# First weights on ScalarE's queue, attention's bias and the identity behind the first loads, twelve products of ones at the start of a hybrid decoder layer

## The chip, the core and the metric

The kernel runs on one core of one Trainium2 chip (trn2). The core has TensorE (matrix products into PSUM), VectorE (DVE), ScalarE (ACT), GpSimd (POOL) and SyncE (SP), which here only issues transfers; 16 DMA engines move data between the device's memory and SBUF. Each engine runs its own list of instructions in order and waits on semaphores for the others. The metric is the time of one execution in microseconds (us), the median of the runs.

## What is computed

One layer of a decoder on x with 2048 positions and 1024 channels, float32 throughout. Cut to what matters here:

```python
h = rmsnorm(x, norm1_g)
z = h @ w_in            # columns: q | k | v | conv a, gate | lru gate, x
y_attn = attention_mixer(q, k, v)      # 6 heads, three dilated windows, ALiBi bias
y_conv = conv_module(...)              # GLU, causal depthwise conv of 31 taps, LayerNorm, swish
y_lru  = recurrent_mixer(...)          # gated linear recurrence
x = x + concat(y_attn, y_conv, y_lru) @ w_out
x = x + square(relu(rmsnorm(x, norm2_g) @ w_up)) @ w_down
return rmsnorm(x, final_g)
```

## The kernel before, in words

The 2048 positions are done in two halves of 1024. For each half the input projection runs (`inproj`), then the three mixers, the output projection and the two large products of the MLP. Tensors lie with channels on the 128 partitions. A float32 product is made of three products of rounded parts: every operand is split by `split` into a rounded high part (ScalarE, a cast or a scaled copy, lines 235 and 238) and a low part (VectorE, lines 236 and 239), and `products` (lines 255, 258, 261) multiplies high by high, high by low and low by high. Each such product is 128 rows by 512 columns.

`inproj(0)` begins the program. x arrives as eight rows of 128 channels (k = 0 to 7), each in two blocks of 512 positions (256 KB, line 329), the weights as blocks of 128 x 512 (256 KB, line 244 in `load_w`). All of these pass through five raw buffers in turn (`raw_tile`), so that a load waits until the block that had its buffer is split. The split weights go to a ring of eight tiles (`wide_ring`), so that a cast can wait for TensorE to be done with older weights. The first group of `project` multiplies three column tiles of w_in with all eight rows: 18 products for each row k, into six PSUM banks. Beside the split, ScalarE squares each block (lines 266 and 269) and VectorE adds the squares (line 270); when row 6 comes up, `norm` multiplies these sums with the matrix `ones_d` (line 279, a plain float32 product), and square root (line 351), reciprocal (line 352) and the evacuation of the banks (line 381) follow. Only then can the second group have its bank.

The first weight block is asked for by `acts.between`, which the first pass of `Acts.more` calls once, after the first activation block. The order of the rest on each engine is set by a scheduler that knows the program's order and the priorities given in it; `tc.issue_after` holds an instruction behind another.

Ahead of `inproj`, `body` loads `vec` (all small vectors), sets `ones_d` on GpSimd and a few constants. `project_v` (line 397 on) loads the identity for transposes (`ident`, line 399); it is used first there, at line 404. `setup` prepares the recurrence's small weights and a polynomial on VectorE (lines 217 to 231). `attention` takes its bias (the ALiBi slopes and masks, 128 x 512) from `consts` by `bias_of` (line 644) on GpSimd's queue, and then the first unit's queries, keys and values by `fetch_keys` (lines 591, 606, 610), which come back from the device's memory (`zscr`, `vscr`) and so wait for their stores. The bias is added to the scores at line 711 on VectorE. The taps of the convolution (line 462) run on VectorE in the same stretch.

Of the kernel before, what the change touches and what calls it, by code (L numbers as in the profile page):

```python
# [77 lines left out]
def body(tc, xt, w_in, w_v, w_out, w_up, w_down, vecs, lru_wa, lru_wx, consts, out):  # L78
# [114 lines left out]
    def v(name, i=0, n=1):  # L193
        at = VEC[name][0] + i
        return vec[:, at:at + n]

    def setup():
        for m, w in enumerate((lru_wa, lru_wx)):
            raw = wide_tile()[:, :3 * P]
            nc.gpsimd.memset(raw, 0.0)  # L200
            for t in range(3):
                for j in range(2):
                    nc.sync.dma_start(raw[j * HD:(j + 1) * HD, t * P + j * HD:t * P + (j + 1) * HD], w[2 * t + j])
            gh, gl = X(22)[:, m * 3 * P:(m + 1) * 3 * P], X(23)[:, m * 3 * P:(m + 1) * 3 * P]
            split(raw, gh, gl)
            for part, a in ((m, gh), (2 + m, gl)):
                nc.sync.dma_start(gates_w.rearrange("t p n -> p t n")[:, :, part * P:(part + 1) * P],
                                  a.bitcast(F32).rearrange("p (t n) -> p t n", t=3))
        zero = cst.tile([P, 32], F32, name="zero")
        nc.gpsimd.memset(zero, 0.0)  # L210
        for t in range(2):
            nc.sync.dma_start(uscr[t][:, 0:32], zero)
        for t in range(3):
            nc.sync.dma_start(lscr[t][:, 0:32], zero)
        lam = v("lru_lambda", 0, 3)
        w = [splus[:, 3 * i:3 * i + 3] for i in range(5)]
        nc.scalar.activation(w[0], lam, AF.Abs)
        nc.scalar.activation(w[0], w[0], AF.Exp, scale=-1.0)
        nc.vector.tensor_scalar(w[1], w[0], 2.0, None, op0=OP.add)
        nc.vector.reciprocal(w[1], w[1])  # L220
        nc.vector.tensor_tensor(w[0], w[0], w[1], OP.mult)
        nc.vector.tensor_tensor(w[1], w[0], w[0], OP.mult)
        nc.vector.memset(w[2], 1.0 / 19)
        for n in range(17, 0, -2):
            nc.vector.tensor_tensor(w[2], w[2], w[1], OP.mult)
            nc.vector.tensor_scalar(w[2], w[2], 1.0 / n, None, op0=OP.add)
        nc.vector.scalar_tensor_tensor(w[2], w[2], 2.0, w[0], op0=OP.mult, op1=OP.mult)
        nc.vector.tensor_scalar(w[3], lam, -1.0, 0.0, op0=OP.mult, op1=OP.max)
        nc.vector.tensor_add(w[2], w[2], w[3])
        nc.vector.tensor_scalar(w[3], w[2], 8.0, None, op0=OP.mult)  # L230
        nc.vector.tensor_scalar(w[4], w[2], -8.0, None, op0=OP.mult)
# [6 lines left out]
            nc.scalar.activation(h, raw, AF.Copy, scale=scale)  # L238
            nc.vector.scalar_tensor_tensor(l, raw, scale, h.bitcast(F32), op0=OP.mult, op1=OP.subtract)

    def load_w(src):
        n = src.shape[-1]
        raw = raw_tile()[:, :n]
        nc.sync.dma_start(raw, src)
        h, l = wide_ring()[:, :n], wide_ring()[:, :n]
        split(raw, h, l)
        return h, l
# [48 lines left out]
    def project(src, group, acts, nk, evac, hook=None):  # L296
        banks = [[main_bank() if i < 2 else mix_bank() for _ in range(2)] for i in range(len(group))]
        w = {}
        if not len(acts):
            acts.between = lambda: w.update({0: load_w(src(group[0], 0))})  # L300
        for k in range(nk):
            while len(acts) < k + 1:
                acts.more()
            if hook is not None and k == hook[0]:
                hook[1]()
            for i, t in enumerate(group):
                if k % 4 == 0 and (k or i not in w):
                    w[i] = load_w(src(t, k // 4))
                products(banks[i], w[i], k % 4, acts[k], k == 0, k == nk - 1)
            while len(acts) < (min(k + 2, nk) if k < 4 else nk):  # L310
                acts.more()
        for i, t in enumerate(group):
            evac(t, banks[i])
# [3 lines left out]
    def inproj(h, after=None):  # L317
# [78 lines left out]

        def project_v():
            if h == 0:
                nc.sync.dma_start(ident, consts[:, 6 * 256:])
            nc.sync.dma_start(rscr[tok].rearrange("(a n) -> a n", a=1), r1[0:1, :])  # L400
            rows = raw_tile()[0:8, 0:P]
            nc.sync.dma_start(rows, rscr[tok].rearrange("(c p) -> c p", p=P))
            bank = (main_bank if h else conv_bank)()
            nc.tensor.transpose(bank[:, 0:HS // P], rows, ident[0:8, 0:8])
            nc.scalar.copy(rcol[h], bank[:, :HS // P])
            for c0 in range(0, HS // P, 4):
                banks = [main_bank()[:, :VW] for _ in range(4)]
                for k in range(KT):
                    wh, wl = load_w(w_v[k])
                    ah, al = acts[k]  # L410
                    for i, bank in enumerate(banks):
                        c = slice((c0 + i) * P, (c0 + i + 1) * P)
                        nc.tensor.matmul(bank, ah[:, c], wh, start=k == 0, stop=False)
                        nc.tensor.matmul(bank, ah[:, c], wl, start=False, stop=False)
                        nc.tensor.matmul(bank, al[:, c], wh, start=False, stop=k == KT - 1)
                for i, bank in enumerate(banks):
                    c = c0 + i
                    if i % 2 == 0:
                        z = z_tile()
                    o = z[:, i % 2 * NB:i % 2 * NB + VW]  # L420
                    nc.vector.tensor_scalar(o, bank, rcol[h][:, c:c + 1], None, op0=OP.mult)
                    nc.sync.dma_start(vscr[h * HS + c * P:h * HS + (c + 1) * P, :], o)
# [158 lines left out]
    def fetch_keys(h, g, bt, half):  # L581
        load = attn_loads(h).dma_start
        c0 = h * HS + bt * NB + half * 256
        back = (P, NB, HS)[g]
        own = slice(c0, c0 + 256)
        lead = 0 if c0 < back else P if g == 0 else 256
        width = lead + 256
        raw = mtile()[:, :NB]
        for a in range(2):
            ap = slice(a * HD, (a + 1) * HD)  # L590
            load(raw[ap, :].rearrange("p (j n) -> p j n", j=2), zscr[Q_T + g][:, own].rearrange("(j p) n -> p j n", j=2))
        lows = []
        for j in range(2 if lead else 1):
            kl = mtile_r()[:, :width if lead else NB]
            lows.append(kl)
            rows = slice(j * HD, (j + 1) * HD)
            for a in range(2):
                dst = kl[a * HD:(a + 1) * HD, :].bitcast(F32)
                if g == 0 and lead:
                    load(dst, zscr[K_T + g][rows, c0 - lead:c0 + 256])  # L600
                elif lead:
                    at = c0 // back * back
                    src = zscr[K_T + g][rows, at - back:at + back].rearrange("p (b n) -> p b n", b=2)
                    load(dst.rearrange("p (b n) -> p b n", b=2), src[:, :, c0 - at:c0 - at + 256])
                else:
                    load(dst.rearrange("p (j n) -> p j n", j=2), zscr[K_T + g][:, own].rearrange("(j p) n -> p j n", j=2))
        vv = mtile()[:, :width]
        vc = slice(g * P, (g + 1) * P)
        if g == 0:
            load(vv.rearrange("p (b c) -> p b c", c=P), vscr[c0 - lead:c0 + 256, vc].rearrange("(b p) c -> p b c", p=P))  # L610
        else:
            for at, t in ((lead, 0),) + (((0, back),) if lead else ()):
                dst = vv[:, at:at + 256].rearrange("p (u c) -> p u c", u=2)
                if g == 1:
                    base = h * HS + bt * NB - t
                    src = vscr[base:base + NB, vc].rearrange("(s r) c -> s r c", r=4)
                    load(dst, src[:, 2 * half:2 * half + 2, :])
                else:
                    base = h * HS - t
                    src = vscr[base:base + HS, vc].rearrange("(s r e) c -> s r e c", r=8, e=2)  # L620
                    at_r = bt * 4 + half * 2
                    for e in range(2):
                        load(dst[e * HD:(e + 1) * HD], src[:, at_r:at_r + 2, e, :])
        return raw, lows, vv, lead
# [13 lines left out]
    def attention(h):  # L638
# [3 lines left out]
        def bias_of(g):  # L642
            b = mtile()[:, :NB]
            attn_loads(h).dma_start(b, consts[:, g * NB:(g + 1) * NB])
            return b

        bias = bias_of(0)
        got = fetch_keys(h, *sets[0])
        yield 0
        yield 0  # L650
        qs, keys, vv, lead = split_keys(*got)
# [977 lines left out]
```

## Time and profile before

| | us |
|---|---|
| median of 3 runs | 2007.19 |
| the three runs | 2004.91, 2007.19, 2007.31 |
| profiled execution | 2004.13 |
| its span, first to last instruction | 2002.3 |
| TensorE busy in the span | 1953.0 (98%) |
| VectorE busy | 1447.3 (72%) |
| ScalarE busy | 1041.1 (52%) |

All rows come from the one profiled execution; its times count from the span's start. In the rows PE is TensorE and PEld its weight load, DVE is VectorE, ACT ScalarE, POOL GpSimd and SPq the queue of SyncE. L255 is line 255 of the kernel before. `raw<-in_xt` names the written and the read tensor. The end of a product is modelled, since products overlap in the array; the distance from one start to the next is what TensorE needs for one. Behind an arrow stands what ended the engine's idle time.

### The profile page before, as it was taken

What the parts mean: (1) busy time and instruction counts of PE and PEld (TensorE: products, weight loads), DVE (VectorE), ACT (ScalarE), POOL (GpSimd) and SP (SyncE); (2) the same over time, 40 slices, a digit from 0 to 9 for tenths busy, and PEclk for the clock granted to TensorE, in tenths of its full rate; (3) what the DMA queues carried; (4) which work ended last, traced back from release to release, by engine and by line L of the source; (5) the groups of instructions that cost most, each with busy time, mean ns of one, the idle gap of its engine ahead of it and who ended that gap; (6) DMA issues with size and microseconds to landing.
All of it is one profiled execution on the core that took longest, in us unless ns stands there. A gap on an engine that the chain in (4) does not pass through costs nothing.

```text
span 2002.3 us, 25415 instructions
## 1 busy us (share of the span) xinstructions
PE 1953.0 (98%) x8876; PEld 1588.9 (79%) x8876; DVE 1447.3 (72%) x1961; ACT 1041.1 (52%) x1606; POOL 168.0 (8%) x296
## 2 busy tenths in 40 slices
PE   8999999999999999999999999999999999999996
PEld 6887777877777777888888888787888887888885
DVE  7899783589667666878879899767556555577885
ACT  6144872453557764555565666345555546444441
POOL 0023100100022413000000000100000000000001
PEclk9999999999999999999999999999999999999999
DMA  5555595743656647545888687754444437776773
GB/s 169 164 151 162 168 300 180 245 138 111 202 158 182 194 146 235 176 153 178 277 290 297 208 301 241 241 189 142 148 147 158 150 139 266 250 281 211 273 233 125
DMA packets 201851, 399.51 MB, mean 200 GB/s; under 512 B 25366, under 2 KB 33798, under 8 KB 201660
## 3 DMA queue, kind: packets, MB, share of 16 engines
q1 hardware_dynamic: 182308, 341.49, 50.9%
q0 software_dynamic: 16208, 45.91, 7.7%
q10 hardware_dynamic: 3208, 10.49, 1.5%
q8 instruction: 70, 1.15, 0.2%
q14 instruction: 57, 0.47, 0.1%
HBM read 287.21 MB, written 119.00 MB: 203 GB/s over the span
## 4 chain that ended last, share of the span: by engine, by line
PE 73%; DMA 9%; DVE 9%; ACT 5%; issue 3%; POOL 0%; SPq 0%; DVEq 0%; ACTq 0%; POOLq 0%
PE bank L1120 9%; PE bank L1121 9%; PE bank L1122 9%; PE bank L1419 8%; PE bank L1421 8%; PE bank L1420 8%; PE mm L255 3%; PE mm L261 3%; PE mm L258 3%; PE bank L933 2%; PE bank L935 2%; PE bank L934 2%; DVE rounded L893 1%; DVE wide L462 1%; DMA second<-in_w_down 1%
## 5 line engine op out<-in xcount | busy, mean ns | idle before, releaser
L1120 PE MATMUL bank<-rounded,pair 128*128 128x512 f32 x896 | 353.0, 394 | 3.4 <-ACT low L1129 1.7
L1121 PE MATMUL bank<-rounded,pair 128*128 128x512 f32 x896 | 349.3, 390 | 0.0
L1122 PE MATMUL bank<-rounded,pair 128*128 128x512 f32 x896 | 349.1, 390 | 0.0
L1419 PE MATMUL bank<-rounded,rounded 128*128 128x512 f32 x736 | 288.0, 391 | 2.0 <-DVE z L1432 0.9
L1421 PE MATMUL bank<-rounded,rounded 128*128 128x512 f32 x736 | 286.7, 390 | 1.5 <-DVE rounded L893 1.5
L1420 PE MATMUL bank<-rounded,rounded 128*128 128x512 f32 x736 | 286.4, 389 | 0.0
L893 DVE TENSOR_TENSOR rounded<-rounded 128x1024 fp32r<-128x1024 f32 (+1 forms) x172 | 186.8, 1098 | 74.7 <-ACT rounded L892 73.9
L892 ACT CAST rounded<-rounded 128x1024 fp32r<-128x1024 f32 (+1 forms) x172 | 160.5, 948 | 133.1 <-DMA rounded<-fscr 94.9
L1120 PEld LDWEIGHTS bank<-rounded,pair 128*128 128x128 f32 x896 | 168.2, 188 | 41.4 <-issue 3.0
L1122 PEld LDWEIGHTS bank<-rounded,pair 128*128 128x128 f32 x896 | 168.2, 188 | 35.2 <-issue 0.2
L1121 PEld LDWEIGHTS bank<-rounded,pair 128*128 128x128 f32 x896 | 168.3, 188 | 34.0 <-issue 0.7
L255 PE MATMUL mm<-rounded,rounded 128*128 128x512 f32 x496 | 160.0, 397 | 11.2 <-ACT rounded L235 7.6
L1419 PEld LDWEIGHTS bank<-rounded,rounded 128*128 128x128 f32 x736 | 138.2, 188 | 33.4 <-issue 1.9
L1421 PEld LDWEIGHTS bank<-rounded,rounded 128*128 128x128 f32 x736 | 138.1, 188 | 31.3 <-DVE rounded L893 2.3
L1420 PEld LDWEIGHTS bank<-rounded,rounded 128*128 128x128 f32 x736 | 138.1, 188 | 29.1 <-issue 0.5
L261 PE MATMUL mm<-rounded,rounded 128*128 128x512 f32 x496 | 159.1, 396 | 0.0
L892 ACT CAST rounded<-kept 128x1024 fp32r<-128x1024 f32 x80 | 84.0, 1050 | 144.1 <-DVE kept L1288 72.3
L258 PE MATMUL mm<-rounded,rounded 128*128 128x512 f32 x496 | 157.1, 394 | 0.0
L235 ACT CAST rounded<-raw 128x512 fp32r<-128x512 f32 (+1 forms) x96 | 55.6, 583 | 150.2 <-PE mm L258 92.5
L892 ACT CAST pair<-wraw 128x1024 fp32r<-128x1024 f32 x64 | 67.4, 1053 | 120.0 <-PE bank L1121 113.5
L893 DVE TENSOR_TENSOR rounded<-kept,rounded 128x1024 fp32r<-128x1024 f32 x80 | 97.9, 1223 | 38.4 <-ACT rounded L892 38.0
L893 DVE TENSOR_TENSOR pair<-wraw,pair 128x1024 fp32r<-128x1024 f32 x64 | 78.2, 1222 | 63.2 <-ACT pair L892 61.0
(327 smaller groups left out, 3618.6 us busy)
## 6 DMA issues: line engine op xcount, KB each, us to landing
fscr<-low SPq DMA_DIRECT2D x224, 256.0 KB, 2.1
rounded<-fscr SPq DMA_DIRECT2D x112, 512.0 KB, 4.1
second<-in_w_down SPq DMA_DIRECT2D x80, 512.0 KB, 5.5
kept<-in_w_down SPq DMA_DIRECT2D x48, 512.0 KB, 5.0
raw<-in_w_in SPq DMA_DIRECT2D x64, 256.0 KB, 3.8
low<-in_w_up SPq DMA_DIRECT2D x64, 256.0 KB, 3.2
wraw<-in_w_up SPq DMA_DIRECT2D x64, 256.0 KB, 2.9
raw<-in_xt SPq DMA_DIRECT2D x32, 256.0 KB, 3.7
```

The lines of the kernel that those rows point to most:

```text
L235: nc.scalar.copy(h, raw)
L255: nc.tensor.matmul(bank, wh[:, sl], ah[:, cols], start=first_, stop=False)
L258: nc.tensor.matmul(bank, wh[:, sl], al[:, cols], start=False, stop=False)
L261: nc.tensor.matmul(bank, wl[:, sl], ah[:, cols], start=False, stop=last_)
L892: nc.scalar.copy(h, raw)
L893: nc.vector.tensor_sub(l, raw, f32(h))
L1120: nc.tensor.matmul(bank, wh[:, sl], hi(x), start=fresh and k == 0, stop=False, **kw)
L1121: nc.tensor.matmul(bank, wh[:, sl], lo(x), start=False, stop=False, **kw)
L1122: nc.tensor.matmul(bank, wl[:, sl], hi(x), start=False, stop=k == KH - 1, **kw)
L1419: nc.tensor.matmul(banks[j], th[:, c], sh[:, x], start=fresh and k0, stop=False, **kw)
L1420: nc.tensor.matmul(banks[j], th[:, c], sl[:, x], start=False, stop=False, **kw)
L1421: nc.tensor.matmul(banks[j], tl[:, c], sh[:, x], start=False, stop=k1, **kw)
```

## The change

`body` gets twelve products of `ones_d` with itself (128 columns each, plain float32) into the bank of `conv_bank`, ahead of everything else on TensorE. `load_w` is cut in two: `load_raw` takes a buffer and issues the load on a given queue, and the first weight block is asked for on ScalarE's queue before the activations are, so that it also takes the first raw buffer. The load of the identity is held behind the last activation load. In `attention`, the first bias is asked for after the first unit's `fetch_keys`, and held behind GpSimd's last instruction so far; this holds for both halves.

```diff
+    warm = conv_bank()
+    for _ in range(12):
+        nc.tensor.matmul(warm[:, :P], ones_d, ones_d, start=True, stop=True)
...
+    def load_raw(src, queue):
+        raw = raw_tile()[:, :src.shape[-1]]
+        queue.dma_start(raw, src)
+        return raw
+
+    def load_w(src, raw=None):
         n = src.shape[-1]
-        raw = raw_tile()[:, :n]
-        nc.sync.dma_start(raw, src)
+        if raw is None:
+            raw = load_raw(src, nc.sync)
...
         if not len(acts):
-            acts.between = lambda: w.update({0: load_w(src(group[0], 0))})
+            raw = load_raw(src(group[0], 0), nc.scalar)
+            acts.between = lambda: w.update({0: load_w(src(group[0], 0), raw)})
...
             if h == 0:
-                nc.sync.dma_start(ident, consts[:, 6 * 256:])
+                with tc.issue_after(last_x[0].ins):
+                    nc.sync.dma_start(ident, consts[:, 6 * 256:])
...
-        bias = bias_of(0)
         got = fetch_keys(h, *sets[0])
+        with tc.issue_after(next(i for i in reversed(nc.cur_bb.bb.instructions) if i.engine == mybir.EngineType.Pool)):
+            bias = bias_of(0)
```

On ScalarE at the start of the program, before (`raw_99` and `raw_101` are the two blocks of row 0, `raw_100` the first weights; line 235 casts weights, line 238 rounds activations):

```order
L183 ACT_TABLE_LOAD
L183 ACTIVATE ones_cr<-ones_d 128x128
L217 ACTIVATE splus<-vec 128x3
L218 ACTIVATE splus<-splus 128x3
L238 ACTIVATE rounded_77<-raw_99,vec 128x512
L266 ACTIVATE row_104<-raw_99 128x512
L235 CAST rounded_83<-raw_100 128x512
L238 ACTIVATE rounded_77<-raw_101,vec 128x512
```

The same place now (`raw_99` holds the first weights, `raw_100` and `raw_101` row 0; lines 239 and 242 are the former 235 and 238):

```order
L247 DMA raw_99<-in_w_in 128x512
L183 ACT_TABLE_LOAD
L183 ACTIVATE ones_cr<-ones_d 128x128
L221 ACTIVATE splus<-vec 128x3
L239 CAST rounded_83<-raw_99 128x512
L242 ACTIVATE rounded_77<-raw_100,vec 128x512
L275 ACTIVATE row_104<-raw_100 128x512
L242 ACTIVATE rounded_77<-raw_101,vec 128x512
```

The weights' load stands first, their cast ahead of the first activation block, and the second small operation of `setup` has moved behind the blocks.

On GpSimd around the first attention unit's fetch, before (`in_consts` is the bias):

```order
L210 MEMSET zero 128x32
L644 DMA m<-in_consts 128x512
L591 DMA m<-zscr 64x2x256 x2
L606 DMA mr<-zscr 64x2x256 x2
L610 DMA m<-vscr 128x2x128
L591 DMA m<-zscr 64x2x256 x2
```

The same place now (lines 602, 617, 621 and 655 are the former 591, 606, 610 and 644):

```order
L214 MEMSET zero 128x32
L602 DMA m<-zscr 64x2x256 x2
L617 DMA mr<-zscr 64x2x256 x2
L621 DMA m<-vscr 128x2x128
L655 DMA m<-in_consts 128x512
L602 DMA m<-zscr 64x2x256 x2
```

The bias has moved from the head of the queue to behind the fetch of the values.

## Rows read from the trace of the kernel before

**Rows 1.** The page, busy time of TensorE; then shares of the chain.

```profile
PE 1953.0 (98%) x8876; PEld 1588.9 (79%) x8876; DVE 1447.3 (72%) x1961; ACT 1041.1 (52%) x1606; POOL 168.0 (8%) x296
...
PE 73%; DMA 9%; DVE 9%; ACT 5%; issue 3%; POOL 0%; SPq 0%; DVEq 0%; ACTq 0%; POOLq 0%
```

**Rows 2.** The chain in order of time, 0 to 60: start, us, what.

```profile
2.12 5.57 DMA raw<-in_xt
...
8.49 0.80 PE mm L255
9.29 0.85 PE mm L258 x2
...
14.29 0.47 PE mb L258 x2
...
15.22 0.47 PE mm L255 x2
...
35.65 0.86 PE mb L279 x2
...
45.86 0.47 PE mm L255
```

**Rows 3.** Timeline, 0 to 16: start, us, engine, line, operation, idle before.

```profile
0.74 0.20 POOL L182 MEMSET ones_d<- 128x128 f32 x1 [0.29 <-POOLq L1621]
...
1.72 0.68 POOL L644 DMA_DIRECT2D m<-in_consts  x1
...
5.48 0.72 ACT L238 ACTIVATE rounded<-raw,vec 128x512 fp32r<-128x512 f32 x1 [2.23 <-DMA raw<-in_xt]
6.11 0.61 ACT L266 ACTIVATE row<-raw 128x512 f32<-128x512 f32 x1
...
6.63 0.60 ACT L235 CAST rounded<-raw 128x512 fp32r<-128x512 f32 x1
...
7.07 8.12 SPq L329 DMA_DIRECT2D raw<-in_xt  x8
...
7.28 0.28 PEld L255 LDWEIGHTS mm<-rounded,rounded 128*128 128x128 f32 x1 [7.28 <-ACT rounded L235]
7.28 0.79 PE L255 MATMUL mm<-rounded,rounded 128*128 128x512 f32 x1 [7.28 <-ACT rounded L235]
...
10.60 0.72 ACT L238 ACTIVATE rounded<-raw,vec 128x512 fp32r<-128x512 f32 x1 [0.61 <-DMA raw<-in_xt]
...
12.77 0.75 DVE L239 SCALAR_TENSOR_TENSOR rounded<-raw,vec,rounded 128x512 fp32r<-128x512 f32 x1
```

**Rows 4.** Windows: length, busy (instructions) of PE, PEld, DVE, ACT, POOL; granted clock, DMA.

```profile
10.00:11.00 1.00, 1.00 (x4) 0.81 (x3) 0.98 (x3) 0.40 (x1) 0.00 (x0) 1.00 0.72 219
16.00:17.00 1.00, 1.00 (x6) 0.84 (x5) 1.00 (x3) 1.00 (x3) 0.00 (x0) 1.00 0.72 213
100.00:150.00 50.00, 49.97 (x273) 40.43 (x273) 46.09 (x82) 21.72 (x53) 11.98 (x21) 1.00 0.52 152
150.00:200.00 50.00, 49.28 (x248) 37.42 (x247) 46.80 (x82) 21.68 (x59) 17.47 (x29) 1.00 0.55 161
200.00:250.00 50.00, 48.26 (x237) 37.17 (x236) 36.37 (x72) 43.01 (x80) 9.33 (x16) 1.00 0.57 169
```

**Rows 5.** DMA, 0 to 10: rate in 40 slices; issues with us to landing.

```profile
GB/s 0 0 0 0 0 0 0 149 64 107 180 180 115 115 172 139 229 270 188 164 270 311 385 402 377 377 410 385 393 414 361 299 256 262 195 189 221 320 229 148
...
m<-in_consts POOLq DMA_DIRECT2D x1, 256.0 KB, 5.5
...
vec<-in_vecs SPq DMA_DIRECT2D x1, 58.0 KB
```

**Rows 6.** Timeline, 32 to 36: the last sums of squares.

```profile
34.01 1.29 DVE L270 TENSOR_TENSOR row<-row,tmp 128x512 f32<-128x512 f32 x2
```

**Rows 7.** Timelines of GpSimd and VectorE: third fetch of the first unit, first bias.

```profile
97.84 0.72 POOL L610 DMA_DIRECT2D m<-vscr  x1 [12.94 <-DMA vscr<-z]
...
101.00 0.28 DVE L711 CUSTOM_DVE_ANT_0 m<-mb,m 128x128 f32<-128x128 f32 x1
```

More of the change, by code (lines that the diff above doesn't have):

```diff
@@ L239, in split @@
             nc.vector.scalar_tensor_tensor(l, raw, scale, h.bitcast(F32), op0=OP.mult, op1=OP.subtract)
-    def load_w(src):
+    def load_raw(src, queue):
[3 more added lines that the diff above has]
+    def load_w(src, raw=None):
         n = src.shape[-1]
-        raw = raw_tile()[:, :n]
-        nc.sync.dma_start(raw, src)
+        if raw is None:
+            raw = load_raw(src, nc.sync)
         h, l = wide_ring()[:, :n], wide_ring()[:, :n]
```

## The prediction

> **What bounds the kernel now.** I read the page first: TensorE is busy for 98% of the span of 2002.3 us, and of the chain that ended last 73% is TensorE [rows 1]. So time is lost or won only where TensorE stands still or runs slowly, and the change works at the one place where it does both, the start. The chain in order of time shows it [rows 2]: it begins with the landing of the second half of the first activation block (issued at 2.12, 5.57 us on the way), then TensorE takes over at 8.49 and keeps the chain almost without a break to the second group of products at 45.86. From 9.29 two products of 512 columns take 0.85 us, 0.427 each, which is 512 columns at 1.2 GHz; from 14.29 they take 0.47 and soon 0.45, the 2.4 GHz level. The granted clock of the windows says 1.00 in both stretches, but 4 products start in the us from 10 and 6 in the us from 16 [rows 4]: here the level is read from the spacing, not from that column. TensorE had stood for 7.28 us, made one product, waited again, and then run back to back since 8.49 when the level rose.
>
> The timeline gives the order of arrival [rows 3]: the first activation block is rounded on ScalarE at 5.48, the first weights behind it at 6.63, the first product at 7.28. The second activation row is issued at 7.07, lands at 10.60, and its last low part is done by VectorE at 12.77 + 0.75 = 13.5. At the slow level TensorE reaches that row only at 15.22 [rows 2], 1.7 us after it was ready: TensorE, not the data, set the pace.
>
> **Part 1, first weights on ScalarE's queue; bias and identity away from the start.** Before, vec (58 KB), the first block, its weights, the bias (256 KB, landed 1.72 + 5.5 = 7.2) and three further blocks share the DMA engines, and about 585 KB have moved by 5.25 (the first 21 slices of the rate row, a quarter us each) [rows 3, 5]. After, the first 570 KB are vec, first weights and first activation block alone. At the same rates both have landed by 5.25; the weights are issued at about 0.74, where ScalarE now starts with a table load, so I take 4.9 for them and 5.3 for the block. ScalarE casts the weights (0.60) to 5.5 and rounds the block (0.72) to 6.2 [rows 3]: first product at 6.25, against 7.28. The bounds are 5.6 (all landed at 4.3) and 6.9 (both at 5.5, as the first block now).
>
> The Trainium skill speaks against more: in "Trainium Kernel Development and Optimization", Key Constraints, it says that transfers issued from several engines' queues run on the same 16 DMA engines and interleave, so a second queue saves issue time only. By that rule weights and block would land together at about 5.3 and the first product would be at 6.65; the sum below would lose 0.4 us.
>
> The buffer of the first weights takes the second activation row next. It is free at 4.9 + 0.60 + 0.75 = 6.25, against 7.07 now; with the 3.53 us from issue to use of now [rows 3] the row is there at 9.8. Round, square, round (0.72, 0.61 to 0.65, 0.72) end at 11.9, VectorE's low part at 12.65. Small set-up operations are pushed behind the blocks on VectorE; they have no reader near, and I cost them at nothing.
>
> **Part 2, the twelve products of ones.** A plain f32 product of 512 columns takes 0.86 at the fast level [rows 2], so one of 128 columns 0.215, or 0.43 at the slow one. Twelve last 2.6 to 5.2 us. They wait for ones_d alone (0.74 + 0.20 [rows 3]) and so end between 3.5 and 6.1, ahead of the first product at 6.25, and PSUM's bank is next used far behind. Now the level rose after 5.4 us of unbroken work. If it rises for the ones as it did for the products, products run at 0.228 from the start. 18 products per row then take 4.1 us: TensorE would be through the first row at 10.4, and at 10.7 with the third weights' cast. It waits for the second row: two products from 11.95 and the low part at 12.65 make that row start effectively at 12.2. Now it is 15.22: **3.0 us earlier**.
>
> **What is late next.** Row 7 of the first group waits for the sums of squares: VectorE ends them at 34.01 + 1.29 = 35.3 [rows 6], and TensorE arrives at 35.65 [rows 2], with almost no slack. TensorE at 15.22 - 3.0 would arrive at 32.65. Are the sums ready? Their last activation block uses a buffer that a weight block frees, and that weight's cast waits for TensorE to let go of a weight tile; this limb moves by the 3.0. The activations' own stream on ScalarE and VectorE moves by 13.5 - 12.65 = 0.85 only, so the sums come between 32.3 and 34.45, and the product of the sums moves by 1.2 to 3.0. I take 2.4, nearer to the upper end because the last block is freed by weights. From that product to the next group (square root, reciprocals, evacuation; 35.65 to 45.86 [rows 2]) nothing is changed, so the 2.4 us reach the second group.
>
> **Part 3, bias and identity behind.** The identity goes out behind the last activation load, some 50 us ahead of its first use: nothing. GpSimd asked for the bias at 1.72 and stood idle after; now it asks behind the third fetch of the first unit, which was issued at 97.84 after waiting 12.94 for vscr [rows 7]. So it goes out at 97.84 + 0.72 - 2.4 = 96.2 and lands 3.5 (like an activation row) to 5.5 us later, 99.7 to 101.7. VectorE's first use was at 101.00; in the new order it stands behind one more conv tap (about 1.3 us), so it is wanted at 99.9. VectorE stands 0 to 1.8 us. It is busy 46.1 of 50 us there [rows 4] and TensorE waits for nothing: I cost it at nothing, with up to 1.8 in the range. On TensorE the first attention products move back by a few dozen products and the two orders agree again some 590 products in (about 130 us). The second half's bias is asked for over 100 us ahead of its use.
>
> **The sum.** -2.4 us (-1.2 to -3.0; with the bias, +0.6 to -3.0), all on the chain. The profiled execution took 2004.13, which would become 2001.7. It is 3.1 us under the median of the runs, 2007.19, and the three timed runs average 2006.5; from that: **2004.1 us**. What this kernel's measurement can tell from no change is about 0.2%, 4 us.
>
> **Rivals.**
> - *The ones don't raise the clock.* They keep TensorE busy only in short records; the row for it would be 0.427 spacing after the first product. Then the first row takes 18 x 0.427 = 7.7 from 6.25, the second row starts at about 14.3, 0.9 earlier: 2005.6. For it: one product at 7.28 and a wait did not raise it [rows 2, 3]. Against: twelve in a row are unbroken. In "TensorE: Matmul & The Clock Gate", Part 1, the Trainium skill says that the number of slow products differs from run to run and isn't to be fitted; no single trace here can show that.
> - *The bias comes late* (ends slower). VectorE stands in order before the casts' low parts and evacuations, so TensorE is held. For it: the bias was there some 94 us ahead and now has hardly any slack. Against: VectorE's stall comes to 1.8 us at the bounds above. It decides from the point where the bias lands 2.4 us behind the 99.9 at which it is wanted (6.1 us after its issue) and all of that reaches TensorE: then the gain is gone. At 3.1 us behind, the time is 2006.5 + 0.7 = 2007.2.
> - *The ones overrun* (also slower). If each record paid its weight load and its stream one after the other at the slow level (0.28 [rows 3] + 0.21, 24 records), they would end at 12.8, the second row would start at 16.9, 1.7 later: 2008.2. Against: loads of 0.28 hide behind products now.
> - *More is won later.* TensorE idles 0.7 and 1.7 us in 150 to 250 [rows 4], waiting on attention; the new order may close most of it: 2002.1.
>
> **How the numbers follow.** Forecast 0.57, clock stays slow 0.15, bias late 0.08, overrun 0.08, more won later 0.12. The forecast's own range is 2002.3 to 2005.9 (its bounds and about 1 us of scatter). To leave out no more than 2 in 10, the range reaches from 2001.4 to 2007.4. Faster by over 0.2% is below 2003.2: a third of the forecast (0.19) and nearly all of the last rival (0.11), 0.30. Slower by over 0.2% is above 2011.2: only an overrun worse than priced, 0.03. Within: 0.67.
>
> **What would show it.** Right: spacing of 0.228 at the first products, first product at 5.6 to 6.9, second row at about 12.2, sums' product at 32.6 to 34.5, second group at 43 to 44.7, and all later stages as much earlier. Wrong: 0.427 after 8 us; ones that end behind 6.9; a wait of VectorE at the first attention unit that TensorE then shares; a later stage whose wait grows by what the start won.

## The result, and the profile after

| | before | after |
|---|---|---|
| median of 20 runs each, us | 2006.85 | 2013.07 |
| lowest to highest | 2002.62 to 2012.79 | 2004.89 to 2020.99 |
| profiled execution | 2004.13 | 2016.86 |
| its span | 2002.3 | 2015.1 |
| TensorE busy | 1953.0 | 1963.1 |

The changed kernel is slower: ratio 1.0032, 95% interval [1.0023, 1.0042], about 6.2 us. The forecast of 2004.1 and its range are missed. The two profiled executions differ by 12.7 us, twice as much as the medians: the one of before is 2.7 us below its median, the one of after 3.8 us above its own. Rows of single profiles therefore show where time goes; what it costs is taken from the medians and ratios below.

The page's busy times and the shares of the chain, the lines that answer to [rows 1]:

```profile
PE 1963.1 (97%) x8900; PEld 1597.7 (79%) x8900; DVE 1447.8 (72%) x1961; ACT 1040.8 (52%) x1606; POOL 167.8 (8%) x296
...
PE 69%; DMA 11%; DVE 10%; ACT 5%; issue 4%; SPq 0%; DVEq 0%; POOL 0%; ACTq 0%; POOLq 0%
```

TensorE is busy for 10 us more. About 5.5 of them are the twelve products of ones themselves; the rest of its work is the same. Its share of the chain has gone from 73% to 69%, and DMA, VectorE and "issue" took that over. TensorE's timeline at the start (start, us, engine, line, operation, idle time before it), against [rows 2, 3]:

```profile
0.99 5.49 PE L199 MATMUL cb<-ones_d 128*128 128x128 f32 x24 [0.99 <-POOL eps_r L185]
6.80 0.49 PE L264 MATMUL mm<-rounded,rounded 128*128 128x512 f32 x1 [0.32 <-ACT rounded L242]
...
10.40 0.61 PE L264 MATMUL mb<-rounded,rounded 128*128 128x512 f32 x2
10.85 0.62 PE L267 MATMUL mb<-rounded,rounded 128*128 128x512 f32 x2
...
11.76 0.61 PE L264 MATMUL mm<-rounded,rounded 128*128 128x512 f32 x2
...
32.16 1.04 PE L288 MATMUL mb<-row,ones_d 128*128 128x512 f32 x2
```

Pairs of products are 0.45 apart, 0.228 each: the 2.4 GHz level within the first row. The second row starts at 11.76 instead of 15.22, and the sums' product at 32.16 instead of 35.65. The chain of waits shows what became of these 3.5 us:

```profile
32.62 0.60 DVE rounded L240
...
37.19 3.31 DVE row L362 x2
40.51 3.07 issue
43.58 0.64 DVE z L391
...
44.35 0.47 PE mm L264
```

In the gap behind 32.62 VectorE's timeline has twenty-one set-up operations of `splus`, most of them 0.2 us apart, and the chain runs through them. From ScalarE's and VectorE's timelines, the first square root and, of the set-up operations, the first two and the last:

```profile
34.58 0.69 ACT L361 ACTIVATE row<-mb,eps_r 128x512 f32<-128x512 f32 x1
...
33.14 0.16 DVE L230 TENSOR_SCALAR splus<-splus 128x3 f32<-128x3 f32 x1
33.34 0.17 DVE L229 TENSOR_TENSOR splus<-splus 128x3 f32<-128x3 f32 x1
...
37.03 0.16 DVE L235 TENSOR_SCALAR splus<-splus 128x3 f32<-128x3 f32 x1
37.10 6.56 DVE L362 RECIPROCAL row<-row 128x512 f32<-128x512 f32 x2
```

Before, the same places read

```profile
37.88 0.69 ACT L351 ACTIVATE row<-mb,eps_r 128x512 f32<-128x512 f32 x1
...
38.60 6.57 DVE L352 RECIPROCAL row<-row 128x512 f32<-128x512 f32 x2 [2.71 <-ACT row L351]
```

There the first reciprocal starts 0.03 us behind the end of the first square root (37.88 + 0.69 = 38.57). Now that square root ends at 34.58 + 0.69 = 35.27, and the reciprocals stand behind the set-up operations until 37.10: 1.8 us. (The expectation of e2 below counts from the end of the second square root, 35.85, and so has 1.25.) The second group starts at 44.35, 1.5 us ahead of 45.86.

At the first attention unit (before: [rows 7]) the chain leads through the bias; VectorE waits for it, and TensorE for VectorE:

```profile
93.89 1.89 DMA vscr<-z
...
96.30 0.72 POOL m L621
97.02 4.76 DMA m<-in_consts
...
102.28 0.51 PE mb L721 x2
```

VectorE's row for it, and the one wait of TensorE from 80 to 160 us that was not there before (what waited, for what: total, times, longest):

```profile
101.93 0.29 DVE L723 CUSTOM_DVE_ANT_0 m<-mb,m 128x128 f32<-128x128 f32 x1 [1.19 <-DMA m<-in_consts]
...
PE mb L721 <- DVE stat L723: 1.1, 1, 1.1
```

The same product's start in the one trace less that in the other (the lag of after), followed through the program:

| start in before, us | 27 | 47 | 86 | 160 | 250 | 330 | 372 | 500 | 530 | 640 | 830 | 1260 | 1400 | 1730 | 1980 |
|---|---|---|---|---|---|---|---|---|---|---|---|---|---|---|---|
| lag, us | -3.3 | -1.5 | -1.5 | +0.9 | +1.4 | +2.6 | +3.0 | +4.9 | +8.3 | +9.6 | +10.8 | +12.2 | +11.5 | +13.3 | +12.8 |

TensorE's orders differ only up to about 130 us, but most of the loss stands behind that: at 500 to 530, 640, 1700. There TensorE waits and then runs for a while at the 1.2 GHz level. Of windows (length, busy of PE, PEld, DVE, ACT, POOL; granted clock) this is 505 to 520, first of before, then of after:

```profile
505.00:520.00 15.00, 13.48 (x61) 10.84 (x59) 9.05 (x13) 6.41 (x11) 0.00 (x0) 1.00 0.56 188
```

```profile
505.00:520.00 15.00, 11.98 (x46) 9.51 (x45) 8.50 (x11) 6.93 (x8) 0.00 (x0) 0.89 0.69 234
```

### The profile page after: what moved, and what is told of

Read it like the earlier page. It is cut to its first block, busy times and chain, and to the rows that moved or that the text cites. A ratio compares the mean times of both kernels' runs of the same rounds, so it can differ in the third digit from the quotient of the medians.

```text
span 2015.1 us, 25458 instructions
## 1 busy us (share of the span) xinstructions
PE 1963.1 (97%) x8900; PEld 1597.7 (79%) x8900; DVE 1447.8 (72%) x1961; ACT 1040.8 (52%) x1606; POOL 167.8 (8%) x296
## 4 chain that ended last, share of the span: by engine, by line
PE 69%; DMA 11%; DVE 10%; ACT 5%; issue 4%; SPq 0%; DVEq 0%; POOL 0%; ACTq 0%; POOLq 0%
PE bank L1132 9%; PE bank L1133 9%; PE bank L1134 9%; PE bank L1431 7%; PE bank L1433 7%; PE bank L1432 7%; PE mm L270 3%; PE mm L264 3%; PE mm L267 3%; PE bank L945 2%; PE bank L946 2%; PE bank L947 2%; DMA second<-in_w_down 2%; DMA raw<-in_xt 2%; DVE rounded L905 1%
```

## The experiments

Each is timed against the kernel before on its chip.

### Undoing and doing the bias; the set-up operations

e1, made from the changed kernel:

```diff
+        bias = bias_of(0)
         got = fetch_keys(h, *sets[0])
-        with tc.issue_after(...):
-            bias = bias_of(0)
```

> The changed kernel, with the attention's bias asked for at the head of GpSimd's queue again, as before the change; first weights on ScalarE's queue, identity behind and the twelve products of ones stay. TensorE's order is then that of before from the second row of weights on. Theory A (moving the bias is what costs): the start still reaches the second group 1.5 us earlier, VectorE's wait of 1.19 us for the bias at the first attention unit and the other order around it are gone, and what was lost behind 87 us (the lag of TensorE's products goes from -1.5 to +0.9 by 151 us and on to +12.8 at the end of the profiled run) does not arise: 2006.85 - 1.5 = 2005.4, between 2004 and 2007. Theory B (an earlier start alone disturbs the later waits and the clock, whatever the bias does): 2010 to 2013, with extra stretches at the 1.2 GHz level between 450 and 700 us.

e2, made from the changed kernel: the polynomial of `setup` becomes `softplus`, called ahead of `inproj(0)`; e3 is e2 with the edit of e1.

```diff
+    softplus()
     inproj(0)
```

> The changed kernel, with the small set-up polynomial written ahead of the input projection, so that its operations stand one by one between the first blocks on VectorE and none stands ahead of the reciprocals; bias still behind the fetch. Both theories: in the changed kernel the square roots end at 35.85 and the reciprocals begin only at 37.10, so the second group should come up to 1.25 us earlier, at 43.1 instead of 44.35 (less if the operations slow the blocks). Theory A: all of it is kept, but the loss at the bias stays: 2013.07 - 1.25 = 2011.8. Theory B: nothing is gained in the end, 2012 to 2015.

> Both edits together: polynomial ahead of the input projection and bias at the head of GpSimd's queue, with the rest of the change. TensorE's order is that of before but for the ones. Theory A: the second group at 43.1, 2.75 us ahead of the 45.86 of the kernel before, and all later stages as much earlier: 2006.85 - 2.75 = 2004.1, so faster than both kernels. Theory B: 2010 or more in spite of the earlier start.

e4, made from the kernel before: only the bias moved, as in the change.

> The kernel before, with the bias moved behind the first unit's fetch and nothing else. Theory A: the whole loss without the gain of the start, 2006.85 + 6.2 + 1.5 = 2014.5, at least 2010, with the wait of VectorE for the bias at about 102 us and the other order around it. Theory B: only the wait itself, 1 to 2 us: 2007 to 2009.

| kernel | median, us | ratio to before, interval |
|---|---|---|
| e1 bias back | 2011.56 | 1.0012 [0.9998, 1.0026] |
| e2 polynomial first | 2013.22 | 1.0026 [1.0013, 1.0040] |
| e3 both | 2010.40 | 1.0010 [0.9999, 1.0022] |
| e4 bias alone | 2008.10 | 0.9998 [0.9987, 1.0009] |

Theory A, that the bias is the loss, falls twice: alone it costs nothing that can be measured, and without it the early start isn't ahead: 1.5 to 2.75 us ahead would be ratios of 0.9986 to 0.9993, below both intervals. The polynomial does at its place what was expected of it and a little more (in e2 the reciprocals start at 35.45, 0.03 us behind the first square root, and the second group at 42.71, 1.64 us earlier than in the changed kernel). At the end no gain can be told: e3 stands with e1, e2 with the changed kernel. These two comparisons are each uncertain by 0.17 to 0.18%, 3.5 us, so 1.6 us could hide in them.

At its own place the bias costs in every profile. From 86 to 160 us the lag grows by 2.5 in the changed kernel, 2.4 in e4, 3.7 in e2 and 4.7 in e8 (below), and by 0.1 or less in e1 and e3. VectorE's wait in e2:

```profile
DVE m L725 <- DMA m<-in_consts: 2.5, 1, 2.5
```

In e8 the load takes 5.51 us, TensorE stands for 1.9, and behind the wait its products of 384 columns come at 0.32 us instead of 0.17, as the chain shows:

```profile
98.69 5.51 DMA m<-in_consts
...
104.69 0.51 PE mb L717 x2
105.20 0.18 PE mm L422
105.38 0.23 PE mm L420
105.61 0.32 PE mm L421
```

### Which part, and is it repeatable?

c1 is the kernel before, unchanged. p1 is the kernel before with a single product of ones. e5 and p3 are the same text, the kernel before with the twelve ones:

```diff
+    warm = conv_bank()
+    for _ in range(12):
+        nc.tensor.matmul(warm[:, :P], ones_d, ones_d, start=True, stop=True)
```

e6 is the kernel before with the first weights on ScalarE's queue (the `load_raw` part of the change). e7 is e3 with `range(24)`. e8 is the changed kernel, e9 is e3, each without the ones.

> The kernel before, unchanged, as a control, and for a second profile of it. Its runs so far go from 2002.5 to 2014.5 around 2007.0, and the profile that the prediction was worked out from, 2004.1, lies near the lower end, with TensorE at the 1.2 GHz level only twice before the end (at 345 and 362 us). Theory C (that profile was a lucky one: the typical run of before has some of the same later stretches at 1.2 GHz as the changed kernels): median 2006 to 2008, and a profile that shows a slow stretch near 512, 622 or 790 us and the time near 2007. Theory A or B alone say nothing of it; a median above 2009 would mean that the differences seen so far (2 to 3 us) are no differences.

> The kernel before with the twelve products of ones and nothing else. Theory A (the start shifts all by what it wins): first product at 6.8 to 7.3 us as before, products 0.228 apart at once, the sums' product some 1 to 2 us earlier and the whole as much: 2005 to 2006. Theory B (an earlier start is given back later and the clock falls more often): 2008.5 to 2011. Theory D (the ones end ahead of the first product and TensorE stands, so the level falls back within the first 14 us, and the ones bring little): 2007, with a slow stretch near 10 us.

> The kernel before with the first weights on ScalarE's queue and nothing else; set-up operations then stand ahead of the reciprocals as in the changed kernel. First product about 0.5 to 1 us earlier, at the 1.2 GHz level. Theory A: the level rises as much earlier, the set-up operations cost up to 1.25 us of it: 2006.5 to 2007.5. Theory B, if it is the weights' queue that disturbs what follows: 2009 or more; if it is the ones: 2007.

> As e3 (polynomial first, bias at the head), but with 24 products of ones, which last until about 11.5 us and so hold the first product back to the 1.2 GHz kernel's pace or later; nothing else differs. TensorE never stands between the ones and the products and the second group starts at about 46 to 47, as before. Theory B (e3 is slower than before since an earlier start is given back later): like before or 1 us over it, 2007 to 2008, and less lost to the clock than in e3. Theory E (not the earlier start but the ones or the queue disturb the rest, in whatever place): as e3 or worse, 2010 to 2012.

> The changed kernel without the twelve products of ones; first weights on ScalarE's queue, identity and bias behind stay. Theory of the ones (B or D: they cost 3 to 5 us in the end, the other parts together 0 to 2): 2006.5 to 2009. Theory F (the parts only lose together, or moving the bias costs as much in the changed kernel): 2011 to 2013.

> First weights on ScalarE's queue, identity behind, set-up polynomial ahead of the input projection; no ones, bias at the head as before. The weights alone gave a ratio of 0.999, with the set-up operations ahead of the reciprocals. Theory of the ones: with these out of the way up to 1.25 us more, 2004.5 to 2006.5, a ratio of 0.998 to 0.9995, faster than both kernels. If earlier work on TensorE is given back later whatever brings it: 2007 to 2009.

> The kernel before with a single product of ones of 128 columns ahead of the first product; the order of everything else on every engine is unchanged. It can hardly move TensorE's level. If each build has an offset of its own of some us (theory P), it may come out anywhere from 2004 to 2011; if the offsets measured so far belong to what the kernels do, 2006.5 to 2008.5.

> The kernel before with the twelve products of ones, the same text as the run e5, once more, for its repeatability and a second profile. If the ones cost 3 to 4 us in the whole kernel (theories G, H): 2010 to 2012.5, a ratio of 1.0015 to 1.003. Theory P: 2005 to 2008.

| kernel | ones | bias moved | median, us | ratio to before, interval |
|---|---|---|---|---|
| c1 before again | | | 2007.96 | 1.0000 [0.9989, 1.0010] |
| p1 one product | 1 | | 2005.96 | 1.0003 [0.9991, 1.0015] |
| e6 weights' queue | | | 2006.23 | 0.9990 [0.9978, 1.0001] |
| e9 weights' queue, identity, polynomial | | | 2005.99 | 1.0003 [0.9989, 1.0016] |
| e8 change without ones | | yes | 2010.28 | 1.0019 [1.0005, 1.0033] |
| e5 ones alone | 12 | | 2011.65 | 1.0022 [1.0011, 1.0034] |
| p3 ones alone, again | 12 | | 2011.15 | 1.0031 [1.0018, 1.0044] |
| e7 as e3, 24 ones | 24 | | 2008.83 | 1.0008 [0.9995, 1.0022] |

Of the parts tried alone only the ones cost: 0.22 and 0.31%, repeatably, and a kernel with a single product does not. The traces show that p1 and e5 differ in more than the number of products: with twelve the scheduler also puts a few loads and set-up operations of the first 45 us in another order, and with one it doesn't; no run separates the two. In the changed kernel the parts don't add up. Without its ones (e8) 0.19% of the 0.32% stay, with the bias back (e1) 0.12%, and what the ones add to e8 (0.13%) or to e9 (0.07%, e3) is within the noise. None of the kernels without ones and with the bias in its place is measurably off the kernel before, and none is shown to be faster; e6 comes nearest to it. e7, where the start is as late as before (the lag at 46 us is 0.1), can't be told from e3 by its ratio. Theory F (the parts lose together) is partly true: the bias on top of the weights' queue costs again (e8 against e6, 0.3%, with the identity moved too), which the bias alone (e4) does not; this difference stays unexplained.

c1 gives a second profile of before, and with it two corrections. Against the first profile its products lag as well, by 0.9 us at 500, 2.8 at 530, 5.0 at 1260 and 3.9 at 1980, so about a third of the lag in the table above is the first profile's luck. And its timeline shows the slow products end at 11.48, not at about 14 as in [rows 2]:

```profile
9.79 1.05 PE L261 MATMUL mm<-rounded,rounded 128*128 128x512 f32 x2
10.64 1.00 PE L255 MATMUL mm<-rounded,rounded 128*128 128x512 f32 x2
11.48 0.63 PE L258 MATMUL mm<-rounded,rounded 128*128 128x512 f32 x2
```

In the ten profiles without ones or with a single product of them the first product that is less than 0.25 us from the next comes between 9.9 us (e6) and 14.1 us. The last is the profile that the prediction rests on, so the ones had most to win there.

### Where the ones lose it: three pairs of cut kernels

Each pair is the kernel before and the kernel before with the ones, ended at the same place; up to there every engine has the order of the whole kernel, except for the first pair, where the mixers are missing.

```diff
     inproj(0)
+    for name in reversed(list(pools)):
+        close(name)
+    return
```

cut2 has the same lines behind `inproj(1, between)`, cut3 behind the first `up(...)`.

> The kernel before, ended behind the input projection of the first half: set-up, mixers, second half, output projection and MLP are left out, and the output is not written. It takes some 150 to 200 us, so that each of its runs shows what the start does, and its mean granted clock shows single falls. It is read against the next kernel, not against the whole one. TensorE's level should rise at different times from run to run (the profiles of four kernels without the ones show 9.8 to 14.0 us), so its runs should spread by about 2 us.

> The same cut kernel with the twelve products of ones. Theory D (the ones lose at the start already: TensorE stands between their end and the first products and the level falls back): no faster than the cut kernel before, 0 to 2 us slower, with a lower mean granted clock in many of its runs. Theory B (the start gains and the loss comes later): 1 to 2.5 us faster than the cut kernel before in the median, with hardly a fall of the clock, and the whole loss of 4 us and more of the kernel with ones alone arises behind the first projection.

> The kernel before, ended where the input projections of both halves and the first half's mixers are done: the second half's attention and mixers, output projections and MLP are left out, and the output is not written. Its order on every engine is that of the whole kernel up to there. It takes some 480 to 520 us and is read against the next kernel.

> The same cut kernel with the twelve products of ones. The cut at the first projection showed the ones 1.6 us faster at its end, and the whole kernel with ones alone is 4 us slower: 5 to 6 us have to be lost in between. Theory G (lost at the waits of the second half's projection, near 345 and 362 us): here already no faster than its partner, 0 to 4 us slower. Theory H (lost behind 500 us, at the output projection and the MLP): here still 1 to 2 us faster. Theory P (the whole kernel's 4 us is an offset of that build or chance): here 1 to 2 us faster, and the repeated kernel with ones alone comes out near 2006.

> The kernel before, ended behind the first half's first MLP product: the second product, the second half's output projection and MLP are left out, and the output is not written. Its order on every engine is that of the whole kernel up to there. It takes some 960 us and is read against the next kernel.

> The same cut kernel with the twelve products of ones. At 228 us the ones were 1.7 us ahead, at 518 us 0.8 behind, and the whole kernel ends 4 to 6 behind. Theory H (most is lost at the few places between 500 and 830 us where TensorE stands, at the first half's output projection and MLP, by longer waits and more falls of the clock): here 3 to 5 us slower than its partner. Theory S (the loss goes on to grow over the whole program): 1 to 2 us slower.

| ended at | before: median (range), us | with ones | difference |
|---|---|---|---|
| first projection | 229.71 (229.06 to 229.89) | 228.02 (227.45 to 228.46) | -1.7 |
| second projection | 517.77 (513.34 to 519.93) | 518.59 (516.25 to 520.24) | +0.8 |
| first MLP product | 973.15 (972.14 to 975.55) | 977.44 (972.51 to 982.64) | +4.3 |
| whole kernel (e5, p3) | | | about +4 to +6 |

So the start does win, 1.7 us with no overlap of the runs, and the kernel with ones loses about 6 us between 230 and 970 us, and little or nothing behind that (theory S). By the medians 2.5 us are lost up to 518 us (theory G) and 3.5 from there to 973 us (theory H); the runs of the second pair overlap almost wholly, so this division isn't shown.

The granted clocks of the same runs tell how much of it is the clock. Time lost to it, (1 - mean granted clock) x span in the mean of the runs, is 1.0 us before and 2.6 with the ones in the first pair, 4.6 and 7.2 in the second, 7.5 and 11.9 in the third: 1.6, 2.6 and 4.4 us more with the ones. This is an estimate: it takes half of all time at the 1.2 GHz level as lost, also where TensorE stands, and it leaves out the slow start of before, where the column reads 1.00. Without it the kernel with ones would be 3.3 us ahead at the first cut, 1.8 at the second and 0.1 at the third. So two things happen: what the start won is used up at waits, and the clock takes some 4 us on top.

The 1.7 is what is left at the start after a loss: in the profile of cut_ones the ones end at 6.28, TensorE stands for 1.34 us, and the level falls back within the first row, where pairs come 0.85 apart again (the mean granted clocks of the five runs, 0.986 to 0.992 against 0.993 to 0.997 in cut_before, point to a fall in most of them):

```profile
0.98 5.30 PE L199 MATMUL cb<-ones_d 128*128 128x128 f32 x24 [0.98 <-POOL eps_l L187]
7.62 0.50 PE L259 MATMUL mm<-rounded,rounded 128*128 128x512 f32 x1 [1.34 <-ACT rounded L239]
...
9.98 1.05 PE L259 MATMUL mm<-rounded,rounded 128*128 128x512 f32 x2
10.84 1.05 PE L262 MATMUL mm<-rounded,rounded 128*128 128x512 f32 x2
11.69 1.05 PE L265 MATMUL mm<-rounded,rounded 128*128 128x512 f32 x2
```

The waits of TensorE from 320 to 530 us name the places, first of cut3_before, then of cut3_ones:

```profile
PE cb L552 <- DMA mr<-gates_w: 4.8, 1, 4.8
PE bank L933 <- DVE z L381: 2.4, 1, 2.4
PE mm L413 <- DVE z L379: 1.8, 1, 1.8
```

```profile
PE mm L417 <- DVE z L383: 4.7, 1, 4.7
PE bank L937 <- DVE z L385: 3.3, 1, 3.3
PE cb L556 <- DMA mr<-gates_w: 2.0, 1, 2.0
```

L413 (with the ones L417) begins the products of the second half's values. VectorE evacuates the bank that it needs (L379), and stands in order behind L822, which waits for blocks of the attention's output that go to the device's memory and come back (`oscr`). VectorE's timelines around it, of cut3_before and cut3_ones:

```profile
343.32 0.69 DVE L822 TENSOR_TENSOR m<-m 128x512 f32<-128x512 f32 x1 [4.17 <-DMA m<-oscr]
...
344.39 1.28 DVE L379 TENSOR_TENSOR z<-mm,row 128x512 f32<-128x512 f32 x2
```

```profile
344.90 0.69 DVE L826 TENSOR_TENSOR m<-m 128x512 f32<-128x512 f32 x1 [6.04 <-DMA m<-oscr]
...
345.98 1.28 DVE L383 TENSOR_TENSOR z<-mm,row 128x512 f32<-128x512 f32 x2
```

TensorE comes to this wait at 343.4 in the one and 342.0 in the other, and is let go at 345.1 and 346.7. Behind the short wait its products stay 0.17 to 0.18 apart, behind the long one they are 0.32 apart:

```profile
345.13 0.45 PE L413 MATMUL mm<-rounded,rounded 128*128 128x384 f32 x1 [1.76 <-DVE z L379]
345.41 0.34 PE L414 MATMUL mm<-rounded,rounded 128*128 128x384 f32 x1
345.59 0.33 PE L415 MATMUL mm<-rounded,rounded 128*128 128x384 f32 x1
```

```profile
346.72 0.69 PE L417 MATMUL mm<-rounded,rounded 128*128 128x384 f32 x1 [4.69 <-DVE z L383]
347.20 0.52 PE L418 MATMUL mm<-rounded,rounded 128*128 128x384 f32 x1
347.52 0.52 PE L419 MATMUL mm<-rounded,rounded 128*128 128x384 f32 x1
```

Over six profiles each with the bias in its place (without ones: before, c1, p1, e6, e9, cut3_before; with ones: e5, p3, e3, e1, e7, cut3_ones) the means of when TensorE comes to the wait and when it is let go are:

| wait | without ones | with ones |
|---|---|---|
| values' first product, L413 | 343.1 to 345.6 | 341.9 to 346.0 |
| gates' weights from `gates_w`, L552 | 357.1 to 361.4 | 358.5 to 361.4 |
| output projection's first bank, L933 | 507.7 to 510.3 | 507.7 to 510.8 |
| attention of the second half, L747 | 614.7 to 617.2 | 616.7 to 619.5 |
| MLP, L1120 | 783.8 to 786.1 | 786.6 to 788.8 |

Single profiles lie 1 to 3 us about these means (standard deviation), so differences of 1 to 2 us between the columns are a sign and no proof. The 1.2 us by which TensorE is early at 342 are gone at 361.4, the same time in both: the second wait ends with a load from the device's memory and the first hangs on one, and an earlier TensorE stands there longer. Then, from 508 to 617, the kernels with ones fall 2 us behind though they arrive at 507.7 alike. In four of their six profiles (not in e3 and e7) a stretch at the 1.2 GHz level follows the wait at 508; without ones it is one of six (e6). In all sixteen profiles of whole or nearly whole kernels it follows eight of the ten waits there of 2.8 us or more, and none of the six of 2.4 us or less. Whether and why that wait is longer with the ones (3.1 us against 2.5 in the mean, 1.5 to 3.5 in single profiles of either kind) is not settled: its chain runs through a load of `out_w`, 5.82 us in cut3_before and 6.41 in cut3_ones.

## Why the prediction was wrong, step by step

- **The step that failed is the sum, "-2.4 us ... all on the chain"**: that all later stages move by what the start won. The runs show in its place that the ones' 1.7 us at 228 us are a loss of 4.3 us at 973 us (cut pairs). The prediction's list of what would show it wrong names "a later stage whose wait grows by what the start won", and the means point to two such waits, ending at 345 and 361 us; the clock's 4.4 us are the other part. The prediction's rows on TensorE's waits end at 250 us [rows 4]. The wait at L413 (2.4 us in the profile of before) and the one at L552 (3.5 us) were in the same trace; both hang on loads, and no term of the sum asked whether they move.
- **The start itself** went as predicted, relative to the profile used. First product 6.80 (forecast 6.25, bounds 5.6 to 6.9), second row 11.76 (12.2), sums' product 32.16 (32.6 to 34.5, so a little better), second group 44.35 (43 to 44.7); the ones took 5.49 us, over the upper bound of 5.2. That the second group lies within its bounds is two misses that cancel: the sums' product came 3.5 us earlier instead of 2.4, and 1.8 were lost behind it, where the prediction has "nothing is changed". And that profile had the longest slow start of ten; the pair of cut kernels puts the gain of the ones alone at 1.7, not 2.4 to 3.0. The Trainium skill, "TensorE: Matmul & The Clock Gate", Part 1, says that the time until the level rises differs from run to run; the prediction cited it and then took one trace for the size. Here the slow products ended between 9.9 and 14.1 us in ten profiles.
- **The weights' queue.** In the profile of after the cast of the weights starts at 3.78, a us ahead of the forecast, and the rounding of the block, which waits for its load, at 6.03, 0.7 us behind it. So the first product, which needs both, came at 6.80 and not at 6.25. The prediction weighed a rule of the Trainium skill against its forecast ("Trainium Kernel Development and Optimization", Key Constraints: transfers of several queues run on the same engines and interleave) and worked out from it that the two land together and the first product comes at 6.65. They did not land together, but the first product came nearer to that number. In time e6 shows nothing that can be measured.
- **"Small set-up operations ... I cost them at nothing"** was wrong in its place: 1.8 us ahead of the reciprocals, over half of what had been won up to there. e2 against the changed kernel and e3 against e1 show no cost at the end that can be told. If what they take would be lost at 345 us anyway, that fits; it isn't shown.
- **The bias**: VectorE's wait of 1.19 us lies within the 0 to 1.8 that the prediction gave, and the landing (4.76 us after the issue) within its 3.5 to 5.5; in e2 it was 6.1. The failed step is "TensorE waits for nothing: I cost it at nothing": TensorE waits for the same 1.1 us, and with the new order it is 2.4 to 4.7 us later at 160 us. The rival "the bias comes late" had the mechanism and too high a threshold. Its price at the end is nothing that can be measured alone and 0.16 to 0.3% on top of the other parts (e2 against e3, which is within the noise, after against e1, e8 against e6).
- **The identity** cost nothing, as predicted: in the profile of after it is issued at 25.2, lands 3.4 us later and is first used at 77.2.
- **The clock** was counted as won once. The prediction had no case in which the ones are followed by a new fall (cut_ones, at 10 us), nor one in which longer waits are followed by more of them. Time lost to the clock in a run, estimated as above, is 11.2 us in the mean of 35 runs of before, 14.9 and 14.7 in e5 and p3, 14.0 in the changed kernel. All six kernels with twelve ones lie between 13.9 and 14.9, the six without them (c1 and p1 among them) between 10.4 and 12.1, e7 at 12.9. For e5 and p3 the 3 to 4 us more are most of the 4 to 6 that they lose; the bias alone (e4, 10.4) brings none. The slow start of before isn't in that column, which reads 1.00 there [rows 4].
- **The chances** put 0.03 on slower by over 0.2%. All rivals were priced by what happens ahead of 250 us, so none ended over 2 us behind; a case "the gain is absorbed, and the clock falls more often" was missing.

What stays open: why the kernels with ones are at the 1.2 GHz level for longer, and whether the wait at 508 us is longer with them, and so why the loss goes on behind the point where the gain is gone; why the parts don't add up in the changed kernel; why the bias alone costs nothing although TensorE is as late at 160 us in e4 as in the changed kernel; and whether e6, the weights' queue alone, is faster than before. A version that beats the kernel before was not found.

## What to carry to other kernels

A gain at the start of a long kernel is worth what passes the first wait that does not move. Ask of every wait of the bottleneck engine, up to the end, what releases it: one that ends with a load or a round trip through the device's memory can eat an earlier arrival, as the waits at 345 and 361 us seem to here, and in these kernels the time lost to the clock grew on top. Cutting the kernel at a few places and timing the pairs shows in a handful of runs where a gain is lost, best at an early cut: the runs spread by 0.8 and 1.0 us at 229 us, 4 to 7 at 518, 3 to 10 at 973, and 10 for the whole kernel before. The mean granted clock of the same runs tells the clock's part. One profile of each does not show this, and neither does it give the size of an effect that differs from run to run.

## What the runs showed of the hardware

- The level of TensorE's clock rose at different times in equal or nearly equal starts: slow products ended between 9.9 and 14.1 us in the ten profiles without ones or with one, whose first products came between 6.2 and 8.1.
- Products of ones that end ahead of the first real product do not always hold the level. Of nine profiles with twelve ones it fell again in the first row in three (e1, cut_ones, cut2_ones) and held in six. The three had their first real product at 7.37 to 7.80 us, the six at 6.13 to 6.99; the stand of TensorE ahead of it does not part them (0.9 to 1.9 us against 0 to 1.6).
- The column of the granted clock reads 1.00 while products run at 0.427 us each at the start (c1 from 10 to 11 us, as [rows 4]); the spacing of products told the level.
- The load of 256 KB for the bias took 4.76 us in the changed kernel, 5.51 in e8 and 6.1 in e2, at the same place behind the same fetch on GpSimd's queue, in kernels that differ only in their start.
